# The opening of a decoder trunk on one core: column sums of the modulation in TensorE column groups, six product tiles instead of four, and columns of a later modulation at other places

## The chip, the core and the metric

The kernel runs on one core of a Trainium2 chip. The metric is the device time of one execution in microseconds (us), the median over runs; lower is better. All times in the profile are counted from the start of the profiled span. Engines are called TensorE (PE; its weight loads PEld), VectorE (DVE), ScalarE (ACT), GpSimd (POOL) and SyncE (SP); the last two mostly issue DMA transfers here.

## What is computed

A trunk of two layers, each of them a feed-forward half step, a token mixing and a second feed-forward half step, on 512 rows of 1024 features in float32. What matters for this change is the start of layer 0:

```python
c_act = jax.nn.silu(c)
mod = (c_act @ w_ada[l] + b_ada[l]).reshape(B, N_MOD, D_MODEL)
sh1, sc1, gt1, ... = [mod[:, i, None, :] for i in range(N_MOD)]
hn = rms_norm(h, g_ffn1[l]) * (1.0 + sc1) + sh1
gate, up = jnp.split(hn @ w_in, 2, axis=-1)
h = h + 0.5 * (1.0 + gt1) * ((jax.nn.silu(gate) * up) @ w_out)
```

Before any product of `hn @ w_in`, the kernel needs the root mean square of each of the 512 rows, and from the modulation (a 1024 x 9216 product with one vector, `silu(c)`) the scale `sc1` and the shift `sh1` of the features.

## The kernel before

**Layout.** Features lie on partitions in eight blocks of 128; the 512 rows are the free axis, so block k of the input is a tile `h[k]` of 128 x 512. A float32 product is made from two rounded parts of each operand (`split`, L130 to 135: the high part is a cast on ScalarE, the low part a subtraction on VectorE). `mm3` (L117 to 123) issues three matmuls of 512 columns for one block: high by high, high by low, low by high. In this document a "product" is one such matmul. A tile of the result is eight blocks, so 24 products; its weights are 128 x 1024 floats (0.5 MB) on arrival and are split by one ScalarE and one VectorE instruction.

**Opening** (`begin`, L1143 to 1255). Eight loads bring `h`, one each. While they come in, ScalarE squares and VectorE adds them to `ss`; TensorE sums `ss` over partitions (`ps_ss`), ScalarE and VectorE make `rstd`, and TensorE spreads it over partitions (`ps_rstd`, L1229). The vector `silu(c)` is spread by TensorE and ScalarE to `crep` (L1204, 1205), 128 x 1024. The modulation blocks come in pairs of blocks, 1 MB a load (`fetch`, tile `wada`), between the first four weight tiles (`fetch_w`, tile `wfirst`). A column of the modulation, the sum of one block's 1024 terms for 128 features, is made in one of two ways:

- on VectorE, a product with `crep` with an accumulated sum over 1024 elements (`ada_dot`, L192): the scales, and the shift of the first block of each pair;
- on TensorE, eight matmuls of one column (`ps_ada`, L1180): the shift of the second block of each pair.

`normed` (L1183 to 1188) then makes `z = h * rstd` on VectorE, scale and shift in one ScalarE instruction (`hn_t`), and the two parts `hnH` and `hnL`. Products of four tiles are interleaved with this (the loop at the end of `begin`); warm-up matmuls that nobody reads (`warm`) fill TensorE before. The tiles of VectorE, ScalarE and TensorE work are placed by a scheduler in the order of the program where nothing else is given; `tc.issue_after` puts instructions of one engine behind a given one.

**First feed-forward step** (`ffn`, L337). With `n_first == 4` (only here, in layer 0's first step) sixteen tiles in all are plain products: four from `begin`, twelve more from `projector`. Two tiles, gate and up, make one piece j of the hidden layer: silu on ScalarE (L501), the product on VectorE (L503), and again two parts, the cast on ScalarE (L504) and the low part on VectorE (L505). After that the "paired part" begins (`pair_in`, L428 to 475), which needs fewer multiplications by taking sums of blocks of `hn` and of weights. It starts with these, in this order on its engines:

```python
S = raw(A(1, 0), ("sum0", "sum1")[p % 2])
plus(S, A(1, 1))
first_sum = hl(S)
prod(pF, first_sum, P1, True)
a11 = raw(A(0, 0), "first")
prod(pD, hl(a11, S), B11, True)
```

The products write `ps_f`, `ps_d` and `ps_g`; ScalarE evacuates `ps_f` to `up` (L442) and `ps_d` to `s` (L446). The sums of `hn` are made before, on VectorE, beside the last plain tiles: `x = hnH + hnL` (L388, eight of them), then the combinations P1, P2, T3 and T4 (`combine`, L391 to 410, tiles `q`), each split into `comH` and `comL`. The tiles `q` for P1 and T3 lie in the buffer `first`, so the weight load that `pair_in` puts there (`a11`) waits until T3 is split.

**Columns of the next modulation.** Beside the plain tiles VectorE also makes eleven columns that are wanted later (`ada_steps`, L200 to 217): GpSimd issues a load of 0.5 MB for each, into one of three buffers by turns (`first`, `third`, `sum1`), and `ada_dot` sums it. How many columns stand behind which piece j is the tuple on L508. They use another `crep`, loaded at the start of `ffn` on SyncE (L196) and put through silu on ScalarE (L197). SyncE's queue also issues all weight loads of the plain tiles, in program order, each when its buffer is free.

Of the kernel before, what the change touches and what calls it, by code (L numbers as in the profile page):

```python
# [17 lines left out]
P = 128  # L18
# [14 lines left out]
GAP = 448  # L33
GROUPS = ((0, 12), (12, 22))
# [24 lines left out]
def trunk_kernel(ctx, tc, ins, out, layers=L, phases=("ffn1", "mix", "ffn2")):  # L59
# [57 lines left out]
    def mm3(acc, w, k, x, sl, start, stop):  # L117

        wH, wL, xH, xL = w[0][:, k], w[1][:, k], weave(x[0][:, sl]), weave(x[1][:, sl])
        acc = paired(acc)  # L120
        mm(acc, wH, xH, start=start, stop=False)  # L121
        mm(acc, wH, xL, start=False, stop=False)  # L122
        mm(acc, wL, xH, start=False, stop=stop)  # L123
# [23 lines left out]
    for i in range(KD):  # L147
        t = hp_.tile([P, T], F32, name=f"h{i}")
        nc.sync.dma_start(t, ins["xT"][i])
        h.append(t)  # L150
# [186 lines left out]
    def ffn(l, w_in, w_pair, w_out, hn, im, ss, need, then, first, ready, coming):  # L337
# [6 lines left out]
        with tc.tile_pool(name="act", bufs=1) as ap_:  # L344
# [147 lines left out]
            for g, (j0, j1) in enumerate(GROUPS):  # L492
                for p in range(j0 // 2, j1 // 2):
                    if p < n_first:
                        X = new_x(p)
                        for j in (2 * p, 2 * p + 1):
                            pg = next(tiles)
                            beside(2 * j)
                            pu = next(tiles)
                            s = E("silu")  # L500
                            act(pg.like(s), pg.view, AF.Silu)  # L501
                            for seen, part in pu.pieces(s):
                                stt(part, part, -1.0, seen, ALU.mult, ALU.mult)  # L503
                            nc.scalar.copy(xs[j][0], s)  # L504
# [638 lines left out]
    def begin(pool):  # L1143
# [3 lines left out]
        col = {n: pool.tile([P, KD], F32, name=n, tag=n) for n in ("sc", "sh", "gb", "gm0", "sh0")}  # L1147
        stt(col["gb"], bsc, 1.0, g1, ALU.add, ALU.mult)
        wa, wf, ws = {}, [], []

        def fetch(m):
            for n in (0, 2):
                w = pool.tile([P, 2, D], F32, name="wada", tag="wada", bufs=8)
                nc.sync.dma_start(w, ins["wa0"][m, :, n : n + 2])
                wa[m, n], wa[m, n + 1] = w[:, 0], w[:, 1]

        def fetch_w():
            j, g = divmod(len(wf), 2)
            w = pool.tile([P, KD, P], F32, name="wfirst", tag="wfirst", bufs=4)
            nc.sync.dma_start(w, ins["w1i"][0, j, g])  # L1160
            wf.append(w)

        def split_w(n):
            pair = tuple(wp.tile([P, KD, P], F32R, name=x, tag=x, bufs=4) for x in ("wH", "wL"))
            split(*pair, wf[n])
            ws.append(pair)

        def scales(m):
            for n in range(2):
                k = slice(2 * m + n, 2 * m + n + 1)  # L1170
                ada_dot(col["sc"][:, k], wa[m, n], crep)
                stt(col["gm0"][:, k], col["sc"][:, k], g1[:, k], col["gb"][:, k], ALU.mult, ALU.add)

        def shifts(m):
            k0, k1 = (slice(2 * m + n, 2 * m + n + 1) for n in range(2))
            ada_dot(col["sh"][:, k0], wa[m, 2], crep)
            tt(col["sh0"][:, k0], col["sh"][:, k0], bsh[:, k0], ALU.add)
            pt = psum([P, 1], "ps_ada")
            for k in range(KD):
                mm(pt, wa[m, 3][:, k * P : (k + 1) * P], cact[:, k : k + 1], start=k == 0, stop=k == KD - 1)  # L1180
            tt(col["sh0"][:, k1], pt, bsh[:, k1], ALU.add)

        def normed(k):  # L1183
            z = E("z")
            tt(z, h[k], rstd, ALU.mult)
# [4 lines left out]
        pw = psum([P, T], "ps_warm", "r1")  # L1190
        wide = ones_r.unsqueeze(1).to_broadcast([P, 4, P])

        def warm(n):

            for _ in range(n):
                mm(pw.rearrange("p (a b) -> p a b", b=P), ones_r, wide, start=True, stop=True)

        warm(3)

        crep = pool.tile([P, D], F32, name="crep", tag="crep")  # L1200
        for hf in range(2):
            pt = psum([P, 4, P], "ps_crep")
            for k in range(4):
                mm(pt[:, k], cT[:, 4 * hf + k : 4 * hf + k + 1].to_broadcast([P, P]), cst("ident"), start=True, stop=True)  # L1204
            act(crep[:, hf * 512 : hf * 512 + 512], pt.rearrange("p k n -> p (k n)"), AF.Silu)
        fetch(0)
        fetch_w()
        fetch_w()
        fetch(1)
        fetch_w()  # L1210
        fetch_w()
        fetch(2)
        fetch(3)
        nc.sync.dma_start(con[:, P:], ins["con"][:, P:])
        warm(20)
# [3 lines left out]

        pt = psum([P, NB], "ps_ss")  # L1220
        for b in range(NB):
            mm(pt[:, b : b + 1], ss[:, b * P : (b + 1) * P], ones[:, :1], start=True, stop=True)
        warm(3)
        r = pool.tile([P, NB], F32, name="rstd_t", tag="rstd_t")
        act(r, pt, AF.Sqrt, bias=vals["eps"], scale=1.0 / D)
        nc.vector.reciprocal(r, r)
        rstd = psum([P, T], "ps_rstd", "r0")
        for b in range(NB):
            mm(rstd[:, b * P : (b + 1) * P], r[:, b : b + 1].to_broadcast([P, P]), cst("ident"), start=True, stop=True)  # L1229
        warm(2)  # L1230
        scales(0)
        shifts(0)
        warm(8)
        normed(0)
        split_w(0)
        split_w(1)
        normed(1)
        pts = [psum([P, T], "ps_mm", tag) for tag in ("mm", "mm", "r1", "r0")]
        for m in range(4):
            groups = [(n, 2 * m + k) for k in range(2) for n in range(4)]  # L1240
            if m == 0:
                groups = [(n, k) for n0 in (0, 2) for k in range(2) for n in (n0, n0 + 1)]
            elif m == 3:
                groups = [(n, 6 + k) for n in range(4) for k in range(2)]
            for g, (n, k) in enumerate(groups):
                mm3(pts[n], ws[n], k, hn[k], ALL, k == 0, k == KD - 1)
                if m < 3 and g == 1:
                    scales(m + 1)
                    shifts(m + 1)
                    if m == 0:  # L1250
                        split_w(2)
                        split_w(3)
                    normed(2 * m + 2)
                    normed(2 * m + 3)
# [35 lines left out]
def lay_out(i):  # L1290
# [4 lines left out]
    a["xT"] = c(i["x"][0].T).reshape(KD, P, T)  # L1295
# [5 lines left out]
    last = i["w_ada"][0, :, :D].reshape(KD, P, 4, 2, P)[:, :, :, 1].transpose(2, 1, 0, 3).reshape(4, P, D)  # L1301
    a["wa0"] = c(np.stack([wT[0, 1, ::2], wT[0, 1, 1::2], wT[0, 0, ::2], last], axis=2))
# [68 lines left out]
```

## Time and profile before

| | |
|---|---|
| runs of the kernel | 1866.52 us median of three (1865.02 to 1866.69) |
| the profiled execution's own time | 1866.04 us |
| its span in the profile | 1864.0 us |
| TensorE busy | 1828.7 us, 98% of the span |
| VectorE busy | 1398.4 us, 75% |
| ScalarE busy | 836.3 us, 45% |
| GpSimd busy | 130.9 us, 7% |
| instructions | 33421, of them 13664 matmuls |

The profile was taken from one execution, so its numbers are compared with that execution's own time; that time is 2.0 us more than the span, for what lies before the first and after the last instruction. A matmul record carries a modelled end, and consecutive matmuls overlap, so a busy TensorE is not one at its peak; the granted clock (1.00 is full speed) tells whether it ran at full rate. Rows of groups give busy time, the mean of one instruction in nanoseconds, the idle time of the engine just before, and what ended most of that idle time ("<-"). A float32 matmul whose operands are not rounded before appears as two records.

### The profile page before, as it was taken

To read this page: it belongs to the slowest core of one execution; us is meant where nothing else is said; L and a number is where in the kernel's file an instruction comes from. 1 tells how busy PE (TensorE), PEld (TensorE's weight loads), DVE (VectorE), ACT (ScalarE), POOL (GpSimd) and SP (SyncE) were. 2 spreads that over 40 slices of the span, in tenths; PEclk is the share of its full clock that TensorE was granted. 3 is DMA by queue.
4 is the path that set the end of the run, shared out by engine and by line. 5 is a ranking of instruction groups with operands and counts; after the bars stand their busy time and mean duration, and the time that the engine had idled before them with its cause. 6 is when DMAs were issued, how large, how long until landed. Compare 5 with 4: busy or idle time off the path is not lost.

```text
span 1864.0 us, 33421 instructions
## 1 busy us (share of the span) xinstructions
PE 1828.7 (98%) x13664; PEld 1644.4 (88%) x13664; DVE 1398.4 (75%) x2202; ACT 836.3 (45%) x1272; POOL 130.9 (7%) x212
## 2 busy tenths in 40 slices
PE   8999999999999999999999999999999999999999
PEld 6889899986777999899999988999767788998998
DVE  7687677867986887777878786777589778874872
ACT  4443255346422555245345524544563335532551
POOL 0101110100000000110100020110000000100100
PEclk8999999999999999999999999999999999999999
DMA  7667876621122475886737688773212125775752
GB/s 307 225 185 234 263 197 202 221 83 46 58 55 72 136 195 176 296 223 195 246 112 197 171 272 228 192 229 114 101 56 59 53 68 161 209 227 139 203 144 68
DMA packets 104313, 308.24 MB, mean 165 GB/s; under 512 B 23392, under 2 KB 24416, under 8 KB 103136
## 3 DMA queue, kind: packets, MB, share of 16 engines
q1 hardware_dynamic: 75936, 203.34, 32.3%
q0 software_dynamic: 28224, 102.77, 21.7%
q8 instruction: 107, 1.75, 0.4%
q14 instruction: 46, 0.38, 0.1%
HBM read 302.66 MB, written 3.41 MB: 164 GB/s over the span
## 4 chain that ended last, share of the span: by engine, by line
PE 71%; DVE 13%; DMA 7%; issue 4%; ACT 4%; POOL 1%; SPq 0%; POOLq 0%; DVEq 0%; ACTq 0%
PE ps_mm L121 11%; PE ps_mm L122 10%; PE ps_mm L123 10%; PE ps_d L420 6%; PE ps_d L422 6%; PE ps_d L421 6%; PE ps_f L420 3%; PE ps_f L422 3%; PE ps_f L421 3%; DMA wada<-in_wadaT 2%; DVE wL L135 2%; PE ps_g L422 2%; PE ps_g L420 2%; PE ps_g L421 2%; ACT wH L133 1%
## 5 line engine op out<-in xcount | busy, mean ns | idle before, releaser
L133 ACT CAST wH<-wraw 128x1024 fp32r<-128x1024 f32 (+2 forms) x292 | 266.1, 918 | 434.7 <-PE ps_mm L122 190.2
L135 DVE TENSOR_TENSOR wL<-wraw,wH 128x1024 fp32r<-128x1024 f32 (+2 forms) x292 | 307.2, 1058 | 105.1 <-ACT wH L133 104.4
L123 PE MATMUL ps_mm<-actH,wL 128*128 128x512 f32 (+1 forms) x784 | 281.5, 359 | 2.8 <-DVE wL L135 2.8
L121 PE MATMUL ps_mm<-actH,wH 128*128 128x512 f32 (+1 forms) x784 | 281.6, 359 | 0.0
L122 PE MATMUL ps_mm<-actL,wH 128*128 128x512 f32 (+1 forms) x784 | 281.2, 359 | 0.0
L121 PE MATMUL ps_mm<-hnH,wH 128*128 128x512 f32 (+1 forms) x760 | 267.5, 359 | 5.7 <-ACT hnH L133 2.9
L122 PE MATMUL ps_mm<-hnL,wH 128*128 128x512 f32 (+1 forms) x760 | 266.5, 353 | 0.5
L123 PE MATMUL ps_mm<-hnH,wL 128*128 128x512 f32 (+1 forms) x760 | 266.4, 353 | 0.6 <-DVE wL L135 0.6
L420 PE MATMUL ps_d<-comH,wH 128*128 128x256 f32 x816 | 224.7, 275 | 0.3 <-ACT s L446 0.3
L421 PE MATMUL ps_d<-comL,wH 128*128 128x256 f32 x816 | 224.4, 275 | 0.0
L422 PE MATMUL ps_d<-comH,wL 128*128 128x256 f32 x816 | 224.4, 275 | 0.0
L192 DVE SCALAR_TENSOR_TENSOR wada<-wada,crep 128x1024 f32<-128x1024 f32 x140 | 167.7, 1219 | 48.8 <-DMA wada<-in_wadaT 48.2
L135 DVE TENSOR_TENSOR wL<-sum,wH 128x1024 fp32r<-128x1024 f32 x102 | 124.9, 1224 | 71.5 <-ACT wH L133 71.3
L123 PEld LDWEIGHTS ps_mm<-actH,wL 128*128 128x128 f32 x784 | 149.1, 190 | 20.3 <-DVE wL L135 3.6
L121 PEld LDWEIGHTS ps_mm<-hnH,wH 128*128 128x128 f32 x760 | 143.4, 191 | 24.9 <-issue 3.8
L121 PEld LDWEIGHTS ps_mm<-actH,wH 128*128 128x128 f32 x784 | 149.1, 190 | 16.8
L122 PEld LDWEIGHTS ps_mm<-actL,wH 128*128 128x128 f32 x784 | 149.0, 190 | 16.8
L123 PEld LDWEIGHTS ps_mm<-hnH,wL 128*128 128x128 f32 x760 | 145.5, 191 | 19.3 <-issue 4.3
L122 PEld LDWEIGHTS ps_mm<-hnL,wH 128*128 128x128 f32 x760 | 145.4, 192 | 17.2 <-DVE hnL L277 1.6
L420 PEld LDWEIGHTS ps_d<-comH,wH 128*128 128x128 f32 x816 | 156.7, 192 | 0.9 <-ACT s L446 0.9
L422 PEld LDWEIGHTS ps_d<-comH,wL 128*128 128x128 f32 x816 | 156.7, 192 | 0.0
L421 PEld LDWEIGHTS ps_d<-comL,wH 128*128 128x128 f32 x816 | 156.7, 192 | 0.0
(354 smaller groups left out, 3855.6 us busy)
## 6 DMA issues: line engine op xcount, KB each, us to landing
wada<-in_wadaT POOLq DMA_DIRECT2D x128, 512.0 KB, 4.8
wraw<-in_wmi SPq DMA_DIRECT2D x40, 512.0 KB
wraw<-in_w2p SPq DMA_DIRECT2D x36, 512.0 KB
wraw<-in_w1p SPq DMA_DIRECT2D x32, 512.0 KB
wraw<-in_w1o SPq DMA_DIRECT2D x32, 384.0 KB
wraw<-in_w2o SPq DMA_DIRECT2D x32, 384.0 KB
wraw<-in_w1i SPq DMA_DIRECT2D x20, 512.0 KB
wraw<-in_w1o SPq DMA_DIRECT2D x32, 320.0 KB
```

Of the source, the lines that this page charges most:

```text
L121: mm(acc, wH, xH, start=start, stop=False)
L122: mm(acc, wH, xL, start=False, stop=False)
L123: mm(acc, wL, xH, start=False, stop=stop)
L133: nc.scalar.copy(hi, src)
L135: return nc.vector.tensor_sub(lo, src, hi.bitcast(F32))
L192: stt(w, w, 1.0, crep, ALU.mult, ALU.mult, accum_out=out_)
L420: mm(acc, wH, xH, start=start and i + k == 0, stop=False, skip_group_check=True)
L421: mm(acc, wH, xL, start=False, stop=False, skip_group_check=True)
L422: mm(acc, wL, xH, start=False, stop=k == 3, skip_group_check=True)
```

## The change

1. The rows `h` are loaded in four transfers of two blocks instead of eight of one (same bytes).
2. Blocks 0 to 3 of the modulation arrive as "streams": scale and shift columns of one block side by side, 8 x 256 columns. `streamed` multiplies them on TensorE: eight float32 matmuls, each with a 32-column stationary operand (`cz`, which holds one column of `silu(c)` and zeros) that writes one of four groups of 32 partitions of `ps_ada`, so four groups with two matmuls each. ScalarE copies the result to SBUF (`part`), and `columns` sums over partitions with two one-column matmuls. `finish` makes the scale and the shift on VectorE.
3. Blocks 4 to 7 take scale and shift from two `ada_dot` each (`dotted`). The `crep` for them is loaded and put through silu (behind the high part of block 3) instead of being made with TensorE. The order of all loads is the tuple `WANTED` (0 a modulation block, 1 a weight tile, 2 `crep`).
4. `normed` now scales and multiplies by `rstd` in one VectorE instruction, adds the shift in the cast on ScalarE, and again in the subtraction for the low part on VectorE. `hnH` is made from `z` directly, without `hn_t` between.
5. Six tiles instead of four are multiplied in the opening, in an order written out by hand (`go`): tiles 0 and 1 start with block 0, tile 2 with blocks 0 and 1, tile 3 with blocks 0 to 2, tile 4 with 0 to 4, tile 5 with 0 to 5. `projector` then makes ten.
6. The eleven columns of the next modulation stand behind the pieces 0, 1 and 2 (four, four, three) instead of 2, 3 and 5.
7. Warm-up matmuls: 30, 2, 5, 3 and 3 at five places instead of 3, 20, 3, 2 and 8.

```diff
+WANTED = (0, 1, 0, 1, 0, 1, 0, 1, 2, 0, 0, 1, 0, 1, 0)
-    for i in range(KD):
-        t = hp_.tile([P, T], F32, name=f"h{i}")
-        nc.sync.dma_start(t, ins["xT"][i])
+    for i in range(0, KD, 2):
+        t = hp_.tile([P, 2, T], F32, name=f"h{i}")
+        nc.sync.dma_start(t, ins["xT"][i // 2])
+        h += [t[:, 0], t[:, 1]]
...
-                                ada_steps(ap_, crep, (0, 0, 4, 4, 0, 3, 0, 0)[j], behind)
+                                ada_steps(ap_, crep, (4, 4, 3, 0, 0, 0, 0, 0)[j], behind)
...
-            w = pool.tile([P, KD, P], F32, name="wfirst", tag="wfirst", bufs=4)
+            w = pool.tile([P, KD, P], F32, name="wfirst", tag="wfirst", bufs=5)
...
-        def normed(k):
-            z = E("z")
-            tt(z, h[k], rstd, ALU.mult)
-            x = E("hn_t")
-            act(x, z, AF.Identity, bias=col["sh0"][:, k : k + 1], scale=col["gm0"][:, k : k + 1])
-            split(*hn[k], x)
...
+        for w in WANTED:
+            (fetch, fetch_w, lambda: nc.sync.dma_start(crep, ins["crep"]))[w]()
...
+        def streamed(k, behind):
+            pt = psum([P, 2 * P], "ps_ada")
+            with tc.high_priority():
+                for i in range(KD):
+                    j = slice(i % 4 * 32, i % 4 * 32 + 32)
+                    m = mm(pt[j], cz[:, i], wa[k][:, i * 2 * P : (i + 1) * 2 * P], start=i < 4, stop=i >= 4)
+                    tc.add_manual_dep(m.ins, behind.ins.name, ORDER, reason="column groups run together")
+                    behind = m
+            part = pool.tile([P, 2 * P], F32, name="part", tag="part", bufs=2)
+            latest["part"] = nc.scalar.copy(part, pt)
+            return part, m
+        def columns(k, part, rest=0, behind=None):
+            pt, c = psum([P, 2], "ps_col"), slice(k, k + 1)
+            for i in range(2):
+                m = mm(pt[:, i : i + 1], part[:, i * P : (i + 1) * P], ones[:, :1], start=True, stop=True)
...
+            if rest:
+                warm(rest, m)
+            finish(c, pt[:, :1], pt[:, 1:])
+        def dotted(k):
+            c = slice(k, k + 1)
+            for n, half in (("sc", 0), ("sh", D)):
+                ada_dot(col[n][:, c], wa[k][:, half : half + D], crep)
+            finish(c, col["sc"][:, c], col["sh"][:, c])
+        def finish(c, sc, sh):
+            stt(col["gm0"][:, c], sc, g1[:, c], col["gb"][:, c], ALU.mult, ALU.add)
+            tt(col["sh0"][:, c], sh, bsh[:, c], ALU.add)
+        def normed(k):
+            z, sh = E("hn_t"), col["sh0"][:, k : k + 1]
+            latest["row"] = stt(z, h[k], col["gm0"][:, k : k + 1], rstd, ALU.mult, ALU.mult)
+            latest["high"] = act(hn[k][0], z, AF.Identity, bias=sh)
+            stt(hn[k][1], z, sh, hn[k][0].bitcast(F32), ALU.add, ALU.subtract)
...
+        columns(0, part, 5, last)
+        normed(0)
+        part, m = streamed(1, last)
+        with tc.issue_after(m.ins):
+            last = go((0, 0))
+        columns(1, part, 3)
+        normed(1)
+        split_w(1)
+        last = go((1, 0))
+        part, m = streamed(2, last)
+        last = go((0, 1), (1, 1))
+        columns(2, part, 3)
+        normed(2)
+        split_w(2)
+        last = go((2, 0), (2, 1))
+        part, m = streamed(3, last)
+        go((0, 2), (1, 2), (2, 2))
+        columns(3, part)
+        normed(3)
+        split_w(3)
+        with tc.issue_after(latest["high"].ins):
+            act(crep, crep, AF.Silu)
+        go((3, 0), (3, 1), (3, 2), *((n, 3) for n in range(4)))
+        dotted(4)
+        normed(4)
+        split_w(4)
+        go(*((n, 4) for n in range(4)), *((4, k) for k in range(5)))
+        dotted(5)
+        normed(5)
+        split_w(5)
+        go(*((n, 5) for n in range(5)), *((5, k) for k in range(6)))
+        for k in (6, 7):
+            dotted(k)
+            normed(k)
+            go(*((n, k) for n in range(6)))
```

In `go`, a pair (n, k) is the three products of tile n with block k. The weight tensors' order in memory is changed with it (`lay_out`), so that each load stays one contiguous block per partition.

More of the change, by code (lines that the diff above doesn't have):

```diff
@@ L1174, in shifts @@
[L1174 to L1181, printed above, removed]
-        def normed(k):
-            z = E("z")
-            tt(z, h[k], rstd, ALU.mult)
-            x = E("hn_t")
-            act(x, z, AF.Identity, bias=col["sh0"][:, k : k + 1], scale=col["gm0"][:, k : k + 1])
-            split(*hn[k], x)
@@ L1230, in begin @@
[L1230 to L1233, printed above, removed]
-        normed(0)
-        split_w(0)
-        split_w(1)
[L1237 to L1254, printed above, removed]
+        recip = nc.vector.reciprocal(r, r)
```

84 lines of the change are left out of this document (40 added, 44 removed).

## Prediction

> **What bounds the kernel now.** I read the page first: span, engines, clock.
>
> ```profile
> PE 1828.7 (98%) x13664; PEld 1644.4 (88%) x13664; DVE 1398.4 (75%) x2202; ACT 836.3 (45%) x1272; POOL 130.9 (7%) x212
> ```
>
> TensorE is busy almost always, so an opening can only give back what it loses itself, and only until TensorE next waits. Then the table of stretches, cut where the clock changes and where the seventh product tile and the paired part begin (columns: length, busy time and instructions of PE, PEld, DVE, ACT, POOL, granted clock, DMA share, GB/s).
>
> ```profile
> 15.90:19.40 3.50, 2.35 (x22) 2.26 (x21) 3.40 (x10) 0.60 (x1) 0.00 (x0) 1.00 1.04 432
> 19.40:26.20 6.80, 4.93 (x11) 3.55 (x12) 5.62 (x7) 5.00 (x7) 0.00 (x0) 0.50 1.02 418
> 26.20:29.60 3.40, 2.78 (x21) 2.32 (x19) 3.36 (x11) 0.86 (x2) 0.00 (x0) 0.99 0.99 405
> 29.60:36.40 6.80, 5.86 (x14) 4.69 (x15) 6.72 (x12) 2.74 (x4) 0.00 (x0) 0.50 1.01 413
> ...
> 55.60:117.70 62.10, 62.10 (x289) 54.39 (x288) 49.97 (x72) 24.84 (x32) 6.00 (x10) 1.00 0.66 214
> 117.70:128.90 11.20, 9.00 (x75) 8.40 (x74) 8.80 (x10) 6.56 (x8) 0.86 (x1) 1.00 0.66 149
> ```
>
> Two losses stand there: the opening, with half clock in two stretches of 6.8 us, and 2.2 us of idle at 117.7 to 128.9. Between them TensorE runs without a gap: 62.10 us for 288 products, 0.2156 us each, 5.17 a tile. The waits of that second place are two, and the chain of waits shows what they hang on: VectorE and one load, not TensorE.
>
> ```profile
> PE ps_g L422 <- DVE wL L135: 1.1, 1, 1.1
> PE ps_g L420 <- ACT wH L133: 1.0, 1, 1.0
> ```
>
> ```profile
> 113.84 1.16 DVE comL L135
> ...
> 115.02 3.50 DMA first<-in_w1p
> ...
> 118.59 1.06 ACT wH L133
> ...
> 119.68 1.23 DVE wL L135
> 120.91 1.15 DVE sum L362
> ...
> 122.13 1.07 ACT wH L133
> ...
> 124.97 1.23 DVE wL L135
> ```
>
> The buffer `first` comes free when the combination T3 is split (113.84 + 1.16 = 115.0); its load, two splits and a sum follow in a fixed row to 126.2. So the entry into the paired part stands at a time that VectorE sets.
>
> **The opening, step by step.** Before, the first product starts at 21.12. The fifth tile ends where ScalarE's silu stopped waiting, so the seventh starts a tile later: 61.0 + 5.17 = 66.1.
>
> ```profile
> 11.92 0.69 DVE L235 TENSOR_TENSOR ss<-ss,sq 128x512 f32<-128x512 f32 x1
> ...
> 14.06 0.18 DVE L1226 RECIPROCAL rstd_t<-rstd_t 128x4 f32<-128x4 f32 x1 [1.44 <-ACT rstd_t L1225]
> ...
> 15.52 1.05 PE L1229 MATMUL ps_rstd<-con,rstd_t 128*128 128x128 f32 x8
> ...
> 16.41 1.84 PE L1180 MATMUL ps_ada<-cact,wada 128*128 128x1 f32 x16
> ...
> 16.42 0.35 DVE L1172 SCALAR_TENSOR_TENSOR gm<-sc,par,gb 128x1 f32<-128x1 f32 x2
> ...
> 16.68 0.69 DVE L1185 TENSOR_TENSOR z<-h,ps_rstd 128x512 f32<-128x512 f32 x1
> ...
> 21.12 0.79 PE L121 MATMUL ps_mm<-hnH,wH 128*128 128x512 f32 x1 [2.87 <-ACT hnH L133]
> ...
> 61.05 0.60 ACT L501 ACTIVATE silu<-ps_mm 128x512 f32<-128x512 f32 x1 [0.60 <-PE ps_mm L123]
> ```
>
> Rows in pairs: half as many issues, the same bytes ahead of the first weights; the sum of squares ends as before (12.6), taken as 0, bounds -1 and 0. The load of `crep` and the two more tiles (0.5 MB each) lengthen the opening's list of loads to some 13 MB; at the 405 to 432 GB/s of the first four stretches it ends, by estimate, near 43 us. The first of those two tiles is wanted at 41, so no cost. A new operation is the stream, 8 fp32 matmuls of 256 columns in four column groups. Nearest row: two 64-wide groups of fp32, 512 columns each.
>
> ```profile
> 446.22 1.08 PE L1059 MATMUL ps_av<-pmc,V 128*64 128x512 f32 x4
> ```
>
> ```profile
> L1007 ACT COPY Sc<-ps_sc 128x256 f32<-128x256 f32 x24 | 7.9, 373 | 18.7 <-PE ps_sc L1001 18.7
> L759 ACT ACTIVATE kksq<-k,par 128x512 f32<-128x512 f32 x4 | 2.9, 722 | 0.0
> ```
>
> An fp32 matmul is two records: eight of 128 columns took 1.05 at 15.52, 0.11 each and a tail of 0.17, so a 512-column one takes 0.43. The four of ps_av would take 1.7 and a tail one after another and took 1.08, so groups run together. For a stream: two rounds of two 256-column records, 4 x 0.2156 and the tail, 1.03 us; one after another, 16 x 0.2156 and the tail, 3.6. I take 1.03. A copy of 256 columns out of PSUM is 0.37, two column sums 2 x 0.23 (1.84 for eight), `hnH` in one pass 0.72.
>
> Block 0: the sums end at 13.7, two warm-ups 0.43, stream to 15.2, rstd to 16.2, columns 16.6, two small operations 16.9, z 17.6, first product 18.4: 2.7 earlier than before. But then the order TensorE is given makes a loop: the sums of block k+1 stand behind products of `hnL` of block k, and on VectorE that comes behind a 1.15 us weight split. One round is stream 1.03, copy 0.37, columns 0.46, two small 0.35, z 0.69, split 1.15, `hnL` 0.7 and some products, 5 to 6.5 us: `hnH` of blocks 1, 2, 3 at 22.0, 27.2, 33.7, though their data come every 3.8. Block 4 waits for the silu of `crep`, placed behind block 3's `hnH`.
>
> ```profile
> 54.71 1.06 ACT L197 ACTIVATE crep<-crep 128x1024 f32<-128x1024 f32 x1
> ```
>
> ```profile
> L192 DVE SCALAR_TENSOR_TENSOR wada<-wada,crep 128x1024 f32<-128x1024 f32 x11 | 13.0, 1221 | 0.9 <-DMA wada<-in_wadaT 0.9
> L197 ACT ACT_TABLE_LOAD x1 | 1.3, 1283 | 0.0
> ```
>
> Table and silu to 36.0, three sums of 1.15 (the first half of block 5's stands ahead of z), small 0.3, z, `hnH`: 41.2. TensorE has done 50 of 144 products; 94 x 0.2156 and a wait of 0.7 for a split end at 62.2, 3.9 earlier than 66.1. Blocks 5 to 7 come 5 us apart, covered by those products. That is at full clock. TensorE is on short work or idle through 10 to 34 us; before, 15.90 to 19.40 (2.35 of 3.50 busy) and 26.20 to 29.60 (2.78 of 3.40) were each followed by half clock, and 3.4 us at half cost 1.7 where products are waiting. I take one and 0.4 of waits: seventh tile at 64.3, **-1.8 us** (-4.5 with less waiting, +1.2 with three windows).
>
> **Where the gain goes.** Tiles 7 to 16 are ten times 5.17 in both, so TensorE reaches the paired part at 116.0 instead of 117.8; there VectorE decides. Its list, from the first split that waits for a buffer of the opening's tiles to the split of T3, is before's from 53.4 less three splits, one silu product and one low part.
>
> ```profile
> L135 DVE TENSOR_TENSOR wL<-wraw,wH 128x1024 fp32r<-128x1024 f32 x12 | 14.6, 1223 | 11.0 <-ACT wH L133 10.9
> L388 DVE TENSOR_TENSOR x<-hnH,hnL 128x512 f32<-128x512 f32 x8 | 4.9, 684 | 0.0
> ```
>
> ```profile
> 53.40:84.80 31.40, 31.40 (x147) 27.48 (x147) 20.41 (x28) 15.23 (x20) 2.12 (x4) 1.00 0.62 223
> 84.80:115.00 30.20, 30.20 (x142) 26.44 (x141) 29.20 (x47) 10.73 (x14) 3.87 (x6) 1.00 0.73 222
> ```
>
> ```profile
> 49.19 0.33 SPq L196 DMA_DIRECT2D crep<-in_crep  x1
> ```
>
> ```profile
> DMA to landing us min/median/max: 3.8/5.9/7.4
> ```
>
> Before: 20.41 + 29.20 = 49.6 busy of 61.6, 12.0 idle. After: less three splits (1.2 each) and a silu product and its low part (0.61 each, as the eight x), 49.6 - 4.8 = 44.8. It starts when the first of the six tiles lets its weight buffer go, 1.9 before the seventh tile: 62.4, so T3 is split at 107.2 plus idle. The idle time comes from the moved columns. They now stand at the first three silu tiles, and `crep`, which was asked for at 49 us, stands on SP behind a tile whose buffer frees with that first split (63.5). At 64 to 67 `crep`, three columns and three tiles, 3.7 MB, ask at once; at 0.41 MB/us that is 9 us, and VectorE has 7 us of other work. Every further column waits for one of three buffers (a dot, then a landing of 3.8 to 7.4, the last row above), with splits queued behind the dot. Bounds: 0.7 idle (T3 at 107.9, seven earlier) and before's 12.0 (119.3). I take 8.7, nearer to before's: 115.9, **+0.9** on 115.0. All of TensorE's 1.8 us lead becomes waiting.
>
> Two more costs follow. On VectorE the built order now puts the low split of S ahead of the last tile's silu product; ScalarE's cast of that tile waits for it, and behind the cast stand the evacuations `up` and `s1`, without which the second D product cannot start. Before, the cast had its product and waited for nothing:
>
> ```profile
> 123.09 0.62 ACT L504 CAST actH<-silu 128x512 fp32r<-128x512 f32 x1
> 124.56 0.58 ACT L442 COPY up<-ps_f 128x512 f32<-128x512 f32 x1
> 125.98 0.58 ACT L446 COPY s<-ps_d 128x512 f32<-128x512 f32 x1
> ```
>
> One split, 1.15, less 0.15 of slack: **+1.0** (0 to +1.6). And TensorE, idle 1.8 + 2.2 + 0.9 or so within 7 us, drops to half for one window: **+1.7** (0 to +3.4), by the rows at 19.40 and 29.60, where 67% and 82% busy records did not keep it. From here the two programs are the same but for some reordering at the other entries (a few splits ahead of evacuations): half of the first's cost, **+0.5** (-2 to +3).
>
> Sum: 0.9 + 1.0 + 1.7 + 0.5 = +4.1 on the profiled 1866.04 (span 1864.0), and 0.5 for the median of the runs, 1866.52: **1870.7 us**.
>
> **Rivals.** (1) Faster: the columns land before they are asked for, T3 is split four or more earlier, and the opening's 3.9 at full clock is kept: 1866.5 - 4.1 = 1862.4. For it: landings took as little as 3.8, and VectorE's list alone ends at 107.2. Against: before, VectorE already idled 12 us and its loads stood less crowded. (2) The clock stays full at the entry, as its idle time comes in pieces: 1870.7 - 1.7 = 1869.0. For it: before's entry, 9.00 of 11.20 busy, ran at 1.00 throughout. Against it: at 26.20 to 29.60 only 0.62 of 3.40 was idle, and the next 6.8 us ran at 0.50. [...] (3) The groups do not run together: each stream 3.6, four of them 2.6 longer inside the loop, block 4 and everything behind it 10 later, VectorE's list too: 1880.5, far slower. From 3 us a stream this decides. Against it stands the ps_av row; it has two groups, not four.
>
> **How the numbers follow.** About 0.2% (3.7 us) is what a measurement tells from no change. Forecast 0.42, most of it past that bound (0.30 slower, 0.12 same); rival 1 0.22; rival 2 0.16, same; rival 3 0.12, slower; 0.08 for small shifts either way, half same, half slower. Faster 0.22, same 0.32, slower 0.46. The forecast's own range is 1869 to 1875. The asked range reaches down past rival 1 with the opening's and half the other entries' lower bounds (1866.5 - 4.5 - 1 = 1861) and up over the upper bounds (T3 at 119.3, two windows: 1870.7 + 3.4 + 1.7, and half the other entries' 3): 1861 to 1877.5; rival 3 is left out.
>
> **What would show it.** First product near 18.4 and blocks 1 to 3 five to six apart; four 32-wide matmuls starting together; the seventh tile near 64; `first` issued near 116; more TensorE idle at the entry (4 to 5 us against 2.2) and a half-clock window just after. The prediction is wrong if the seventh tile starts before 62, if T3 is split before 113, or if TensorE crosses the entry without longer waits.

## The result, and the profile after

The changed kernel takes 1872.08 us (median of 20 runs, 1866.95 to 1875.45), the kernel before 1868.02 us in as many runs (1860.21 to 1872.86). The ratio is 1.0023 (95% interval 1.0012 to 1.0033): slower by 4.1 us. The profiled execution of the changed kernel took 1872.61 us, its span is 1870.8 us.

First the opening, in the timeline of the changed kernel (start, duration, engine, line, operation, what it writes and reads; in brackets the wait before it):

```profile
13.78 1.07 PE L1205 MATMUL ps_ada<-wada,cz 128*32 128x256 f32 x16
...
18.48 0.48 PE L122 MATMUL ps_mm<-hnH,wH 128*128 128x512 f32 x1
...
41.63 2.07 PE L122 MATMUL ps_mm<-hnH,wH 128*128 128x512 f32 x4 [2.75 <-ACT hnH L1236]
```

The 16 records of a stream (eight matmuls of two records) take 1.07 us together, where the prediction's estimate for one group after another was 3.6; so the four groups of 32 columns run together. The first products with blocks 0 to 4 start at 18.5, 22.1, 27.6, 34.1 and 41.6. The table of stretches of the changed kernel has one loss of clock in the opening and one behind the entry (columns as in the prediction: length; PE, PEld, DVE, ACT, POOL; clock; DMA share; GB/s):

```profile
29.60:36.40 6.80, 5.49 (x36) 4.19 (x29) 2.80 (x5) 4.38 (x6) 0.00 (x0) 1.00 1.01 415
...
40.00:46.80 6.80, 5.17 (x17) 4.23 (x18) 6.80 (x13) 2.38 (x3) 0.00 (x0) 0.75 0.25 98
46.80:61.00 14.20, 14.20 (x67) 12.45 (x66) 7.39 (x16) 2.09 (x3) 0.00 (x0) 1.00 0.01 1
61.00:115.70 54.70, 54.62 (x253) 47.52 (x252) 45.94 (x67) 22.70 (x29) 7.75 (x13) 1.00 0.78 250
115.70:127.80 12.10, 7.73 (x57) 6.50 (x55) 9.88 (x12) 6.69 (x9) 0.86 (x1) 0.96 0.65 174
127.80:134.60 6.80, 6.80 (x36) 6.80 (x37) 2.51 (x3) 2.42 (x3) 0.00 (x0) 0.57 0.59 214
```

Two things are to be seen. From 46.8 to 61.0 TensorE is full and the DMA engines carry nothing (0.01): the next weight loads wait for buffers (the longest wait of SyncE's queue is 20.3 us, for a split on VectorE), and SyncE issues none before 62.68. And TensorE reaches the paired part at 115.76 instead of 117.77, but then is busy only 7.73 of 12.1 us, and the next 6.8 us run at 0.57 of the clock. Its waits there, from the view of waits:

```profile
PE ps_g L423 <- DVE wL L136: 1.6, 1, 1.6
PE ps_d L421 <- ACT wH L134: 0.8, 1, 0.8
PE ps_d L423 <- DVE wL L136: 0.8, 1, 0.8
PE ps_d L421 <- ACT s L447: 0.7, 1, 0.7
PE ps_g L421 <- ACT wH L134: 0.5, 1, 0.5
```

They add up to 4.4 us, against 2.1 before. What they hang on, in the timelines of SyncE and ScalarE of the changed kernel:

```profile
115.06 0.33 SPq L369 DMA_DIRECT2D first<-in_w1p  x1
...
125.11 0.62 ACT L505 CAST actH<-silu 128x512 fp32r<-128x512 f32 x1 [0.94 <-DVE silu L504]
125.63 1.04 ACT L134 CAST wH<-third 128x1024 fp32r<-128x1024 f32 x1
126.58 0.58 ACT L443 COPY up<-ps_f 128x512 f32<-128x512 f32 x1
127.06 0.59 ACT L447 COPY s<-ps_d 128x512 f32<-128x512 f32 x1
...
144.94 0.58 ACT L443 COPY up<-ps_f 128x512 f32<-128x512 f32 x1
```

The load into `first` is issued at 115.06, as before (115.02), although TensorE came 2.0 us earlier. The copy `s` is 1.08 later than before (125.98). The last row is the copy `up` of the second pair, which serves below as the mark of "the place after the entry". In the kernel before it stands here:

```profile
141.13 0.58 ACT L442 COPY up<-ps_f 128x512 f32<-128x512 f32 x1
```

So the entry costs 3.8 us: 1.1 until the copy `s`, and 2.7 behind it, where the clock is half (0.50 from 127.8 to 131.2). That is nearly all of the 4.1 us between the medians. The entry is read from one execution of each kernel; a second one of the kernel before has the mark at 140.8.

### The profile page after: what moved, and what is told of

Read it like the earlier page. It is cut to its first block, busy times and chain, and to the rows that moved or that the text cites. A ratio compares the mean times of both kernels' runs of the same rounds, so it can differ in the third digit from the quotient of the medians.

```text
span 1870.8 us, 33433 instructions
## 1 busy us (share of the span) xinstructions
PE 1830.3 (98%) x13671; PEld 1640.9 (88%) x13671; DVE 1395.9 (75%) x2195; ACT 832.6 (45%) x1268; POOL 131.0 (7%) x213
## 4 chain that ended last, share of the span: by engine, by line
PE 67%; DVE 13%; DMA 8%; issue 6%; ACT 3%; POOL 1%; SPq 0%; DVEq 0%; POOLq 0%; ACTq 0%
PE ps_mm L122 9%; PE ps_mm L123 9%; PE ps_mm L124 9%; PE ps_d L421 6%; PE ps_d L423 6%; PE ps_d L422 6%; DMA wada<-in_wadaT 4%; PE ps_f L423 3%; PE ps_f L421 3%; PE ps_f L422 3%; DVE wL L136 2%; PE ps_g L423 2%; PE ps_g L421 2%; PE ps_g L422 2%; ACT wH L134 1%
## 5 line engine op out<-in xcount | busy, mean ns | idle before, releaser
L193 DVE SCALAR_TENSOR_TENSOR wada<-wada,crep 128x1024 f32<-128x1024 f32 x136 | 163.7, 1221 | 61.7 <-DMA wada<-in_wadaT 59.9
```

Source lines behind the costliest of these rows:

```text
L193: stt(w, w, 1.0, crep, ALU.mult, ALU.mult, accum_out=out_)
```

## The experiments

Twelve runs in three groups. This table has the readings that all share: when the first load of a moved column is issued (GpSimd), when T3 is split on VectorE, the first product of the paired part (ps_f), the mark after the entry, and the ratio of the times to the kernel before. Times are us from the start of the span of one profiled execution.

| run | column asked | T3 split | ps_f | mark | ratio (95% interval) |
|---|---|---|---|---|---|
| before | 49.5 | 115.0 | 117.8 | 141.1 | 1 |
| before_again | 50.0 | 114.8 | 118.3 | 140.8 | one run |
| after | 64.4 | 115.0 | 115.8 | 144.9 | 1.0023 (1.0012 to 1.0033) |
| cols_alone | 49.1 | 110.5 | 117.4 | 138.1 | 0.9998 (0.9979 to 1.0017) |
| cols_again | 49.3 | 112.7 | 117.6 | 139.8 | 0.9996 (0.9984 to 1.0008) |
| opening_alone | 64.6 | 118.5 | 115.6 | 145.0 | 1.0051 (1.0034 to 1.0068) |
| split_later | 64.8 | 114.9 | 115.8 | 142.9 | 1.0021 (1.0001 to 1.0040) |
| entry_filled | 66.0 | 116.8 | 117.5 | 143.9 | 1.0015 (1.0001 to 1.0030) |
| tile_major | 63.8 | 113.2 | 114.8 | 141.9 | 1.0004 (0.9986 to 1.0021) |
| four_tiles | 53.4 | 112.7 | 117.7 | 139.8 | 0.9996 (0.9973 to 1.0019) |
| four_held | 53.5 | 112.5 | 117.6 | 139.6 | one run |
| t3_third | 63.7 | 114.5 | 115.2 | 142.1 | 1.0014 (0.9999 to 1.0029) |
| major_split_third | 65.2 | 113.1 | 116.2 | 141.2 | 0.9995 (0.9977 to 1.0014) |
| four_all | 53.5 | 112.5 | 117.6 | 140.8 | 0.9997 (0.9982 to 1.0012) |

The interval is 0.10 to 0.23% to either side, 2 to 4 us, so most verdicts below rest on the entry in the profiles, and the ratio is a check on them.

### The change taken apart: columns alone, opening alone

```diff
 # cols_alone: the kernel before; opening_alone: the reverse edit in the changed kernel
-ada_steps(ap_, crep, (0, 0, 4, 4, 0, 3, 0, 0)[j], behind)
+ada_steps(ap_, crep, (4, 4, 3, 0, 0, 0, 0, 0)[j], behind)
```

> The kernel before with nothing but the eleven columns moved (4, 4, 3 behind pieces 0, 1, 2). Theory (the entry into the paired part stands where VectorE splits T3, and the columns take as much of VectorE at either place): tile 7 and the first ps_f as before (66.1 and 117.8), T3 split within 1.5 us of before's 115.0, the copy of s1 (125.98 before) 0 to 1.5 later, the time within 0.1% of before. Rival (the moved columns alone make the slowdown): T3 split 2 us or more later, TensorE idle 2 us more at the entry, the time 3 to 5 us above before.

> The changed kernel with the columns back behind pieces 2, 3 and 5. Theory (VectorE and the buffer first pin the entry, wherever the columns stand): first ps_f at 115.8 as in the changed kernel, T3 split at 113 to 116, the copy of s1 at 125.5 to 127, half clock behind the entry again, the time within 2 us of the changed kernel's. Rival (the opening's 2 us are lost to the moved columns): T3 split by 111.5, the copy of s1 by 124, the time 2 to 4 us below the kernel before.

Both theories missed on T3, and so did both rivals; only the time of cols_alone lies where its theory had it. The moved columns alone bring T3 forward by 4.5 us (2.3 in the second profile, cols_again). The entry then has no wait of TensorE at all, as the stretches of cols_alone show:

```profile
117.70:121.00 3.30, 3.30 (x32) 3.30 (x32) 2.23 (x3) 2.85 (x4) 0.00 (x0) 1.00 0.95 154
121.00:124.40 3.40, 3.39 (x31) 3.19 (x30) 3.40 (x4) 3.10 (x5) 0.00 (x0) 1.00 0.42 161
124.40:127.80 3.40, 3.40 (x33) 3.40 (x32) 1.42 (x2) 1.43 (x3) 0.00 (x0) 1.00 0.91 284
```

The opening alone puts T3 at 118.5, 3.4 later than the full change, and TensorE waits 4.8 us in one piece for the high part of `first`:

```profile
PE ps_d L421 <- ACT wH L134: 4.8, 1, 4.8
```

So where the columns stand does matter to VectorE, and in the other direction than thought: at the first pieces they fill time in which it otherwise waits for the casts of weights (from the first split of an own weight tile to T3's it idles 12.0 us in the kernel before, 8.5 of them before weight splits; in cols_alone 8.5 and 4.1), and it is the opening that makes T3 late. In the full change the two cancel (115.0 and 115.0). At the mark opening_alone is no later than the full change (145.0 and 144.9), although its T3 is: its half clock came earlier (0.50 from 124.4 to 127.8) and was nearly over when the products behind the copy `s` (129.6) began (0.60 from 127.8 to 131.2, 1.00 from there). The ratio of opening_alone is larger than its mark explains (3.9 us of 1868 is 0.21%). Its profile is of its quickest execution (1870.22 us, the median is 1875.25), and where the others lose more stays open.

### The two costs behind T3: the late split, and the clock

```diff
 # split_later: in pair_in, for the first pair; low[0] is the last silu product
-                prod(pD, hl(S), P2, False)
+                with tc.issue_after(low[0].ins) if n_first == 4 and p == n_first else nullcontext():
+                    second_sum = hl(S)
+                prod(pD, second_sum, P2, False)
 # entry_filled, in words: matmuls into a bank that nobody reads, in the order of TensorE
 ps_f (24 products), +3, ps_d (2 products), +3, ps_d (22), +2, ps_g (2), +6, ps_g (4), ps_d with S
```

> The changed kernel; on VectorE the low part of S is split behind the last plain tile's silu product instead of ahead of it. Theory (the cast of that tile and behind it the copies up and s1 wait for one split): the cast's wait of 0.94 goes, the copy of s1 comes 0.8 to 1.1 earlier (126.0 against 127.06), the second D product with it. If the shorter idle time keeps the clock full, 2.7 us more. Time 1 to 4 us below the changed kernel's. Rival (s1 is late for another reason: the split of third ahead of it on ScalarE): the copy of s1 moves by less than 0.3 and the time stays.

> The changed kernel with 14 matmuls that nobody reads in the four gaps of TensorE between the first ps_f and the second D product (3, 3, 2 and 6, 0.2156 us each; 3.0 us of work in 3.6 us of waits). Theory (TensorE's idle time at the entry drops the clock for two windows, 2.7 us): the granted clock stays 1.00 from 118 to 135, the place after the entry is 2.5 us earlier than in the changed kernel, the time 2 to 3 us below it. Rival (the half clock there has another cause, such as the load of the whole chip or what went before): the same half clock at 126 to 133, the time as the changed kernel's or up to 1 us above.

In split_later ScalarE no longer waits before the cast of the last tile, and the copy `s` comes 1.25 earlier (0.8 to 1.1 was expected). These are rows of ScalarE's timeline:

```profile
123.86 0.61 ACT L507 CAST actH<-silu 128x512 fp32r<-128x512 f32 x1
124.38 1.04 ACT L134 CAST wH<-third 128x1024 fp32r<-128x1024 f32 x1
125.33 0.57 ACT L443 COPY up<-ps_f 128x512 f32<-128x512 f32 x1
125.81 0.57 ACT L447 COPY s<-ps_d 128x512 f32<-128x512 f32 x1
```

From T3's split to the copy `s` it is 10.9 us here (114.9 to 125.8) and 11.0 before, against 12.0 in the changed kernel, so the split does cost what was forecast. The mark is 2.0 earlier: the half clock followed again, but for a shorter time (0.51 from 127.8 to 131.2, 1.00 from 131.2). The gain of 1 to 4 us did not show in the time: its 1.0021 cannot be told from the changed kernel's 1.0023.

In entry_filled the clock stays full through the entry:

```profile
121.00:124.40 3.40, 3.24 (x22) 2.38 (x21) 2.37 (x3) 1.41 (x3) 0.86 (x1) 1.00 0.24 95
124.40:127.80 3.40, 3.37 (x20) 2.35 (x18) 2.82 (x3) 2.46 (x4) 0.00 (x0) 1.00 0.89 155
127.80:131.20 3.40, 2.51 (x20) 2.29 (x20) 3.34 (x5) 2.65 (x4) 0.00 (x0) 1.00 0.87 184
```

In that execution the opening had lost 1.7 us more (ps_f at 117.5 against 115.8), T3 was split 1.7 later, and yet the mark is 1.1 earlier than in the changed kernel. From T3's split to the mark it is 27.1 us (116.8 to 143.9) against 29.9 (115.0 to 144.9): the fill saves 2.8. So in the changed kernel the clock fell to 0.50 behind these waits, and here, with most of them filled, it stayed at 1.00; the mark shows what the fall cost. The time, 1.0015, is lower than the changed kernel's by less than the intervals can tell.

### What makes T3 late: tiles, buffers, memory

```diff
 # tile_major: the end of the opening
-        for k in (6, 7):
-            dotted(k)
-            normed(k)
-            go(*((n, k) for n in range(6)))
+        for k in (6, 7):
+            dotted(k)
+            normed(k)
+        go(*((n, k) for n in range(6) for k in (6, 7)))
 # four_tiles: no tiles 4 and 5 in the opening, their weight loads left out of WANTED
-        split_w(4)
-        go(*((n, 4) for n in range(4)), *((4, k) for k in range(5)))
+        go(*((n, 4) for n in range(4)))
 ...
 # t3_third
-                tags.update(P1="first", T3="first")
+                tags.update(P1="first", T3="third")
```

> The changed kernel; the last 36 products of the opening go tile by tile (blocks 6 and 7 of tile 0, then of tile 1, ...) instead of block by block, so that tile 0 gives its weight buffers back about 3.2 us earlier (57 instead of 60.3). Theory A (VectorE's list starts late because six tiles hold all weight buffers until 60): the first split of an own weight tile starts 3 us earlier, at 58, T3 is split 2 to 3 earlier, 112 to 113, the copy of s1 at 124 to 125, the time 2 to 4 us below the changed kernel's. Theory B (it is the memory of the opening's pool, which is given back at 64 with the last two tiles and for which crep and the columns wait): the first split earlier, but the first dot still at 71 to 72 and T3 within 1 us of 115.0, the time within 1 us of the changed kernel's.

> The changed kernel with four tiles in the opening instead of six (twelve from the projector, four weight loads, no weight parts in the opening's pool); streams, row pairs and moved columns stay. Both theories on VectorE's late start (weight buffers held, or the opening's memory held) say: crep and the first columns are asked for at 52 to 56 instead of 64, T3 is split at 109 to 112 instead of 115.0. TensorE starts the seventh tile 2 to 4 later than with six tiles (66 to 68) and reaches ps_f at 117.5 to 119.5, with no wait behind it; the place after the entry is 1.5 to 4 us earlier than in the changed kernel. Rival (the streams themselves, not the six tiles, delay VectorE): T3 at 114 or later, the entry's waits as in the changed kernel.

> The changed kernel; the sum T3 lies in the buffer third instead of first, so the load of a11 into first waits only for P1 (split at 107.4) and the load into third comes after T3 instead. Theory (T3 in the buffer first pins the entry): a11 is asked for at 107 to 109 instead of 115.06, the first D product starts behind ps_f without a wait, the copy of s1 at 121 to 124 instead of 127.06, clock full at the entry, the place after the entry 4 to 7 us earlier than in the changed kernel and below the kernel before. Rival (the wait moves on: third and its sum are late instead): the product with T3 waits 2 us or more, and at 150 the place is within 2 us of the changed kernel's.

> The changed kernel with three of these together: tile by tile at the end of the opening, the low part of S behind the last silu product, T3 in the buffer third. Theory: first ps_f at 115.8, less than 1 us of waits from there to 135, full clock, so the place after the entry is 4 us or more before that of the kernel before, and the time 0.2 to 0.4% below it. Rival: the gain of T3's move alone, no more.

Four tiles instead of six undo the damage at the entry. GpSimd may issue the first column 11 us earlier, and T3 is split at 112.7. This is GpSimd's row in the changed kernel and then in four_tiles:

```profile
64.42 1.77 POOL L207 DMA_DIRECT2D wada<-in_wadaT  x3 [63.36 <-DVE wL L136]
```

```profile
53.43 1.77 POOL L207 DMA_DIRECT2D wada<-in_wadaT  x3 [52.37 <-PE ps_mm L123]
```

The buffers of the columns and of `crep` belong to the pool that follows the opening's, so they come free when the opening's pool (its memory on chip) is read for the last time. The clearer rows are those of SyncE's load of `crep`, which is issued 0.6 us ahead of GpSimd's in both. What it waited for, in the changed kernel and then in four_tiles:

```profile
SPq L197 <- PE ps_mm L124: 0.6, 1, 0.6
```

```profile
SPq L197 <- DVE hnL L1237: 17.8, 1, 17.8
```

With six tiles the weights of tiles 4 and 5 lie in the opening's pool too, and its last reader is TensorE's last product of tile 5, which ends at 63.8; `crep` is asked for at 63.84. (The split on VectorE that the profile names in GpSimd's row ended at the same moment as the row began.) With four tiles the last reader is VectorE's last `hnL`, which reads a shift column until 52.7; `crep` is asked for at 52.85. In tile_major tile 5 ends only a little earlier, and GpSimd's load is issued only a little earlier, at 63.84.

There only the other half is mended: tile 0 gives its weight buffers back earlier, VectorE's first split of an own weight tile starts at 57.6 instead of 61.4, and T3 comes 1.9 earlier (theory A said 2 to 3, B within 1). In four_tiles T3 is 2.3 earlier (2.6 in four_held), a little less than the 3 to 6 that was expected. What each is made of can be counted on VectorE, from its first split of an own weight tile to the end of T3's:

| run | first split | busy | idle | T3 split |
|---|---|---|---|---|
| before | 53.4 | 49.6 | 12.0 | 115.0 |
| cols_alone | 53.1 | 48.9 | 8.5 | 110.5 |
| cols_again | 53.3 | 48.9 | 10.5 | 112.7 |
| opening_alone | 61.6 | 47.2 | 9.7 | 118.5 |
| after | 61.4 | 45.2 | 8.4 | 115.0 |
| tile_major | 57.6 | 45.7 | 9.9 | 113.2 |
| four_tiles | 54.4 | 48.8 | 9.5 | 112.7 |

Idle is the length of the stretch less VectorE's busy time; these are the stretches of after, cols_alone and four_tiles:

```profile
61.40:115.00 53.60, 53.52 (x248) 46.54 (x248) 45.24 (x67) 22.30 (x28) 7.75 (x13) 1.00 0.79 255
53.10:110.50 57.40, 57.40 (x267) 50.27 (x266) 48.91 (x71) 25.51 (x31) 5.98 (x10) 1.00 0.73 238
54.40:112.70 58.30, 58.06 (x268) 50.28 (x267) 48.81 (x71) 23.97 (x30) 6.78 (x12) 1.00 0.77 251
```

Within the list VectorE idles no longer in the changed kernel than in any other of these runs. The list starts 8.3 later than in cols_alone and has only 3.7 less work: that is the 4.5 by which the opening makes T3 late. In tile_major 1.5 us of the earlier start go into longer idle time, as the columns come little earlier. The late start comes from the held weight buffers: in the changed kernel ScalarE's first cast into one of them waits for a product of the opening, and in tile_major, where the same cast may start at 56.5, the list starts 3.8 earlier.

```profile
60.35 1.05 ACT L134 CAST wH<-wraw 128x1024 fp32r<-128x1024 f32 x1 [6.15 <-PE ps_mm L123]
```

What the held memory costs by itself is not shown, since no run keeps six tiles and has the weights of tiles 4 and 5 elsewhere.

The price of four tiles is TensorE's lead: ps_f at 117.7, as before. But almost nothing waits behind it, and the clock stays full: from the copy `s` to the next copy out of `ps_d` it takes 3.6 us, as in four_held, the same kernel, where the clock is 1.00 from 115.6 to 153.0. The view of waits of four_tiles from 100 to 140:

```profile
PE ps_d L421 <- ACT s L447: 0.7, 1, 0.7
PE ps_g L423 <- DVE wL L136: 0.5, 1, 0.5
```

The mark is 5.1 us earlier than with six tiles, more than the 1.5 to 4 that was expected, and the time 0.9996 of the kernel before; its interval (to 1.0019) still meets that of the changed kernel (from 1.0012), so the gain is shown by the entry and not by the time. Taking T3 out of `first` (t3_third) does what it should at its place: the load into `first` goes out at 108.7. But the wait moves on, to the other weights and to ScalarE's copy:

```profile
PE ps_g L421 <- ACT wH L134: 1.6, 1, 1.6
PE ps_d L421 <- ACT s L447: 1.1, 1, 1.1
PE ps_g L423 <- DVE wL L136: 1.1, 1, 1.1
```

The mark moves by 2.8 instead of the expected 4 to 7, and stays behind the kernel before; the copy `s` comes at 125.6 and not by 124. With three edits together (major_split_third) it is at 141.2, where the kernel before has it, and not 4 us ahead: TensorE waits 2.1 us for the next low part there, and from the copy `s` to the next copy out of `ps_d` it takes 5.3 us (124.5 to 129.8), against 3.6 to 3.7 where the clock is 1.00 (before, cols_alone, entry_filled, four_all) and 5.6 in split_later, where it is 0.51.

### A second look at the spread, and a version meant to beat both

```diff
 # four_all: four_tiles, t3_third, split_later, and ahead of block 4
-        go((3, 0), (3, 1), (3, 2), *((n, 3) for n in range(4)))
+        last = go((3, 0), (3, 1), (3, 2), *((n, 3) for n in range(4)))
+        warm(12, last)
```

before_again is the kernel before, cols_again the same kernel as cols_alone, four_held the same as four_tiles.

> The kernel before, profiled a second time. Theory (single half-clock windows at later entries come and go between executions of one kernel): the entry into the paired part as before (ps_f at 117.8, s1 at 126.0, full clock there, within 0.5 us), but other windows later, and the end 1 to 4 us from the first profile's 1864.0. Rival (the windows belong to the kernel): the same two after the opening, at 221 and 1139, and the end within 0.5 us.

> The kernel before with the eleven columns moved, again, with more runs. Theory (its entry into the paired part is 3.1 us earlier and nothing later takes that back): ratio to the kernel before 0.998 to 0.999. Rival (what it gains at the entry is lost at later entries): 0.9995 to 1.001.

> Four tiles in the opening, as in four_tiles, profiled a second time: the opening's half clock at 41 to 46 again, ps_f at 117.7, crep asked for at 52.9 and T3 split by 113. If the entry's waits are under 1.5 us again, the clock stays full there.

> Four tiles in the opening, and three more edits: 12 matmuls that nobody reads before block 4 (TensorE idles 3.2 us there), T3 in the buffer third, the low part of S behind the last silu product. Theory (with the opening's memory given back at 53 VectorE no longer pins the entry, and the clock is held in the opening): no half clock at 41 to 46, ps_f at 115.5 to 116.5, waits under 2 us at the entry, the place after the entry 3 to 4.5 us before that of the kernel before, ratio 0.997 to 0.999. Rival (VectorE pins the entry here too): waits of 2 us or more and half clock at 122 to 130, the place within 1.5 us of the kernel before, ratio 0.9995 to 1.001.

The second profile of the kernel before has the same entry (mark at 140.8, ps_f 0.5 later, `s` 0.35 earlier) and yet a span of 1870.3, 6.3 us more than the first (1 to 4 was expected). A large part is lost where the first lost nothing, at entries near 809 and 1585 (the clock there is 0.75 and 0.74 in the two stretches from 1585.0 to 1591.8, and 1.00 in the first profile). For the former these are the stretches of the first profile and then of the second:

```profile
806.00:809.40 3.40, 2.65 (x23) 2.65 (x24) 3.34 (x4) 1.60 (x3) 0.00 (x0) 1.00 0.31 110
809.40:812.80 3.40, 3.40 (x33) 3.40 (x32) 1.90 (x2) 2.21 (x3) 0.00 (x0) 1.00 0.97 305
```

```profile
806.00:809.40 3.40, 1.78 (x10) 1.59 (x11) 3.40 (x5) 1.99 (x4) 0.00 (x0) 0.87 0.32 120
809.40:812.80 3.40, 3.40 (x22) 3.40 (x22) 2.09 (x2) 0.87 (x1) 0.00 (x0) 0.63 0.63 202
```

So the theory on the spread holds in kind, with a larger spread than expected: such stretches at half clock come and go between executions of one kernel (0.50 from 1139.0 to 1142.4 in the first and 1.00 in the second, too), and two profiles can't be compared by their ends, only stage by stage. (Whether the two executions ran on the same chip is not known.) cols_again has its entry 1.3 us ahead of the kernel before (3.1 in the first look) and a ratio of 0.9996 (0.9984 to 1.0008): within the interval both of a gain of 0.07% and of none. It lies where the rival had it and above the expected 0.998 to 0.999, which the interval does not rule out. four_held repeats four_tiles in every reading of the entry; its span is 3.8 us longer (1869.7 and 1865.9).

four_all holds the clock ahead of block 4 (1.00 from 41.6 to 46.0, where four_tiles has 0.62) but gains nothing by it, ps_f is at 117.6 again: with four tiles blocks 4 to 6 come 3.8 us apart from VectorE's chain of dots, and TensorE waits for them at full clock (2.64 of 3.40 us busy at 1.00 from 44.2 to 47.6) instead of working at half. At the entry, against both the theory's and the rival's account, TensorE waits 2.6 us at full clock and the mark is level with the kernel before; the wait went once more to the next thing, the load into `third`, whose cast stands ahead of both copies on ScalarE:

```profile
124.33 1.04 ACT L134 CAST wH<-third 128x1024 fp32r<-128x1024 f32 x1 [4.14 <-DMA third<-in_w1p]
```

No version is faster than the kernel before by more than the runs can tell.

## Why the prediction was right, and where its reason was not

**The opening, step by step: right.** Predicted starts of blocks 0 to 4: 18.4, 22.0, 27.2, 33.7, 41.2; measured 18.5, 22.1, 27.6, 34.1, 41.6. A stream was put at 1.03 and took 1.07. One window of half clock was taken, and about one came, at 41 behind the wait for block 4 (0.75 from 40.0 to 46.8). The seventh tile was to start at 64.3 and started at 63.6, and TensorE was to reach the paired part at 116.0 and reached it at 115.76.

**The gain becomes waiting: right.** `first` was to be issued near 116 and was at 115.06.

**Why T3 is late: nearly right in size, wrong in the reason for the idle time.** Predicted were a start at 62.4, 44.8 us of work and 8.7 of idle time, T3 at 115.9 and +0.9 us; measured were 61.4, 45.2 and 8.4, T3 at 115.0 and nothing. In the changed kernel most of the idle time stands before the columns:

```profile
L193 DVE SCALAR_TENSOR_TENSOR wada<-wada,crep 128x1024 f32<-128x1024 f32 x11 | 13.3, 1223 | 8.0 <-DMA wada<-in_wadaT 7.7
```

The sentence that failed is "The idle time comes from the moved columns". Put back to their old places (opening_alone) the columns leave 9.7 us of idle time, not less (5.5 before columns, most of the rest before weight splits), and T3 is 3.4 later; moved alone they bring it 2.3 to 4.5 forward. What a wait is put down to did not tell what it would cost to have it gone. Against the kernel before, T3 stands where it stood because three differences cancel: the list starts 8.0 later, has 4.4 less work and 3.6 less idle time. The late start, which the prediction had, is the part that hurts; the columns are among what makes up for it. The prediction also saw the crowd of loads at 64 to 67, but gave the queue behind SyncE's tile and the columns' place as its cause, not the opening's memory that `crep` and the columns wait for.

**The split ahead of the silu product: right.** +1.0 predicted, 1.08 measured at the copy `s`, 1.25 won back when it is undone.

**The clock at the entry: right in kind, too small.** One window of 1.7 was taken; behind the copy `s` the place moved by another 2.7, within the bound of 3.4, and the fill won 2.8.

**The other entries:** +0.5 was taken. The medians differ by 4.1 and the entry by 3.8, which leaves about 0.3, but two profiles of one kernel differ by 6 us there, so this is not measured.

**The sum: its closeness is partly luck.** +4.1 us was forecast and 4.1 measured, with an interval of 2.2 to 6.2. T3's term was 0.9 too high and the clock's 1.0 too low, and the two errors cancel. (Three results in the prediction's text are off by up to 0.2: its sum is 1870.6, T3 with 12.0 of idle time 119.2, and rival 1 with the opening's 3.9 is 1862.6. Nothing hangs on them.)

**The rivals.** (1) fell with T3 at 115.0; its 1862.4 was reached by no run's median. (2) fell with the half clock (0.50 from 127.8 to 131.2): the idle time did come in pieces, the longest of 1.6 us, and the clock fell all the same. In opening_alone a single idle piece of 4.8 us was followed by half clock too (0.50 from 124.4 to 127.8). (3) fell with 1.07 us a stream.

## What to carry to other kernels

A lead on one engine is worth only as much as the next meeting point lets through: find the row that holds that point (here a load behind a buffer that VectorE frees) before counting the gain. When such a list runs late, look at when it starts and how much work it has, and not only at the waits inside it: here the start decided. Work taken into an early stage also keeps that stage's buffers and memory longer, and the loads of the next stage wait for that (here `crep` was asked for at 63.84 with six tiles and at 52.85 with four). When one part of a change is blamed, run that part alone: here the blamed part was one that helped at the entry.

## What was not expected of the hardware

TensorE's clock fell after idle time in small pieces: 1.35 of 3.40 us busy from 123.5 to 126.9 and 1.18 from 124.4 to 127.8, the longest piece 1.6 us, and then 0.50 from 127.8 to 131.2. In four_all a single idle piece of 2.6 us at the same place left it full (1.00 to 132.6), and in the kernel before a stretch with 1.33 of 3.40 busy left it full (1.00 to 129.8). So neither the busy share nor the longest idle piece orders these cases, and what sets the clock here stays open. The rows are of the changed kernel, of the kernel before and of four_all:

```profile
124.40:127.80 3.40, 1.18 (x7) 0.75 (x7) 3.40 (x5) 2.53 (x4) 0.00 (x0) 0.85 0.93 258
127.80:131.20 3.40, 3.40 (x16) 3.40 (x17) 2.51 (x3) 1.04 (x1) 0.00 (x0) 0.50 0.47 167
```

```profile
123.00:126.40 3.40, 1.33 (x10) 0.94 (x9) 3.17 (x4) 3.40 (x6) 0.00 (x0) 1.00 1.01 199
```

```profile
124.00:127.40 3.40, 1.00 (x9) 1.00 (x10) 1.30 (x2) 2.96 (x4) 0.00 (x0) 1.00 0.92 258
```
